# A hybrid decoder block on one core: the mixer's in projection with its column groups in pairs, and seven block products instead of eight for part of them

## The chip, the cores and the metric

The kernel runs on one core of a Trainium2 chip. That core has five engines with instruction streams of their own: TensorE (PE in the profile; its weight loads are PEld), VectorE (DVE), ScalarE (ACT), GpSimd (POOL) and SyncE (SP, which here issues most DMA transfers). Each works through its own list strictly in order and waits at semaphores for the others. The metric is the device time of one execution in microseconds (us).

## The reference, cut to what matters

One layer on 256 tokens of width 2048: a mixer, a cross attention over 256 memory tokens, a gated feed-forward block, each behind an RMS norm and with a residual add. The change lies in the mixer's first product, `proj`:

```python
def hybrid_mixer(h, w_in, ...):
    proj = h @ w_in                       # (256 x 2048) @ (2048 x 11296)
    z, xbc, dt_raw, sc_u, sc_b, sc_c = jnp.split(proj, IN_SPLITS, axis=-1)
    xbc = jax.nn.silu(causal_dwconv(xbc, ssd_conv_w) + ssd_conv_b)
    xs, bm, cm = jnp.split(xbc, ...)
    y = ssd_chunked(xh, dt, a, bm, cm)    # a state space scan, here as 256 x 256 products
    y_ssd = grouped_rmsnorm((y + xh * d_skip) * jax.nn.silu(z), ssd_norm, SSD_GROUPS)
    v = sc_b * causal_dwconv(sc_c * sc_u, sc_conv_w)
    y_sc = grouped_rmsnorm(v, sc_norm, SC_GROUPS)
    return jnp.concatenate([y_ssd, y_sc], axis=-1) @ w_out
```

All arrays are float32.

## The kernel before

**Three products for one.** Each operand of a large product is split into a high part (`fp32r`) and the rest, `hi + lo`, and a block product is three matmuls: hi·hi and lo·hi with the weights' high part (L312, L313 in `tok_mm`), hi·lo with their low part (L316). The weights stream in from memory in chunks of 128 x 1024, which are two feature tiles (a "feature pair") by 512 columns. Each is split when it has landed: ScalarE casts (`h`, L238), VectorE subtracts (`l`, L239). One chunk is then 12 matmuls of 512 columns: two feature tiles, two halves of the tokens (128 each), three matmuls. There are six raw buffers `r`, four of `h` and four of `l`, so a split can be at most four chunks ahead of TensorE.

**The in projection.** Its columns (less 32 that are done apart) are 22 groups of 512. Groups 0 and 1 run together while the input lands; groups 2 to 21 follow one by one, eight chunks each, two chunks to a `unit`. A group has two PSUM accumulators (`a`, four banks in all); the other four banks (`m`, from `msc()`) are lent in turn to the side work.

**Side work.** When a group is summed, its `group_post` starts: scale and evacuate (L338), transpose in blocks (L331), write to memory (`put`) and read back in feature order (`get`), then convolutions, gates, the scan and norms. These are Python generators in a list `procs`; each `unit` calls `step()` once, after its first chunk's matmuls, which moves every one on to its next `yield`. Steps that need TensorE (transposes L717 of a group of `xs`, the scan's products L733 and L735, and others) use banks `m`, which VectorE or ScalarE then read (L720 reads the L717 transposes).

**Who sets the order.** TensorE's and SP's lists stand in the order in which the code is written. VectorE's, ScalarE's and GpSimd's are set once, when the program is built, by a scheduler that may move an instruction far from where it was written. [...]

**Seven products.** Other stages (`wo`, `g`/`u`, `d`) already replace, for some pairs of column groups, the 2 x 2 x 2 block products of a feature pair by seven (a Strassen-Winograd scheme): features in two halves, columns in two groups, tokens in two halves. It needs sums of weight blocks (`pair_sums`: four additions L213 to L216 and three splits L220, L221 a time, on VectorE and ScalarE), sums of token blocks (`token_sums`), four shared PSUM banks `p` for products that go into more than one result, and at the end four additions of these (`p_post`, L938 to L942) and an addition of the correction to each accumulator. `seven_mm` issues 21 matmuls (L990, L991, L993) in three groups: into p[0] and g[0]; into p[3] and p[1]; into p[2], g[1] and u[0].

Of the kernel before, what the change touches and what calls it, by code (L numbers as in the profile page):

```python
# [24 lines left out]
T = 256  # L25
# [5 lines left out]
SEVEN = {n: 3 if n < 10 else 2 for n in range(1, 11)}  # L31
OUT_GAPS = (2, 5, 4, 5)
# [34 lines left out]
def out_order():  # L67

    late = (6, 7, 14, 15)
    return ([(n, c) for n in range(2) for c in range(KT) if c not in late] + [(n, c) for n in range(2) for c in late])  # L70

# [50 lines left out]
def stream_plan():  # L122
# [3 lines left out]
    for n in range(2, 22):  # L126
        p += [(("in", n, c), 1024) for c in range(KT // 2)]
# [8 lines left out]
def trunk(tc, wst, vecs, xp, xtp, mp, mtp, wdt_in, nfin, outp):  # L136
# [9 lines left out]
    with ExitStack() as ctx:  # L146
# [57 lines left out]
        second_of = {part[1]: part[0] for u in out_units() + ffn_units() + down_units() for part in u if len(part) == 2}  # L204
# [129 lines left out]
        def scaled(accs, r):  # L334

            o = [slot() for _ in range(2)]
            for tb in range(2):
                act(o[tb], accs[tb], AF.Identity, scale=r[:, tb:tb + 1])  # L338
            return o
# [40 lines left out]
        def unit(parts, post=None):  # L380
# [192 lines left out]
        def group_post(n, accs):  # L573
            t = turn_blocks(scaled(accs, scales["x"]))
# [15 lines left out]
        def after(k, p):  # L590
            for _ in range(k):
                yield
            yield from p

# [23 lines left out]
        for kt in range(KT):  # L618
            first_unit(kt)

# [231 lines left out]
        def in_units(n, accs, cs):  # L852
            for c in cs:
                unit([([("in", n, k)], lambda k=k: tok_mm(accs, ("in", n, k), side_blocks(xn, 2 * k), (0, 1),
                                                        k == 0, k == KT // 2 - 1)) for k in (c, c + 1)],
                     group_post(n, accs) if c == KT // 2 - 2 else None)

        for n in range(2, len(groups)):
            for one in [] if isinstance(groups[n], tuple) else groups[n]:
                if one[0] == "B" and one[2] > 0:  # L860
                    procs.append(decay(one[2]))
            in_units(n, [acc(), acc()], range(0, KT // 2, 2))
# [68 lines left out]
        shared, seven_a = {}, {}  # L931
        corr = {}

# [19 lines left out]

        def token_sums(key, parts, wide=False):


            xy = fp.tile([128, 1024], F32, tag="f", name=nm("f"))
            w = 512 // len(parts)
            for i, (hi, lo) in enumerate(parts):
# [611 lines left out]
```

## Time and profile before

| | |
|---|---|
| median of 3 runs | 1479.62 us (1479.49 to 1479.84) |
| the profiled execution | 1479.07 us, span of its instructions 1477.3 us |
| TensorE busy | 1466.2 us, 99% |
| VectorE busy | 1212.1 us, 82% |
| ScalarE busy | 864.2 us, 58% |
| DMA moved | 350.91 MB, 238 GB/s on the mean |

The profile is of one execution. A row of a timeline has start, length, engine, line, operation, output tile <- input tiles with shapes, and in brackets how long the engine sat idle before it and on whom it waited. Buffer numbers are left out of names. A row with x4 is four instructions that overlap at their ends, so what one costs in a full list is the distance from start to start. A chain of waits follows the time back from the last instruction, at each step to what released it.

### The profile page before, as it was taken

The page shows a single profiled execution, that of the slowest core. Times are in us where ns is not written, and L with a number is a line of the kernel's source. Part 1 is how long each engine was busy: PE and PEld are TensorE (multiplying, and loading weights), DVE is VectorE, ACT ScalarE, POOL GpSimd, SP SyncE. Part 2 cuts the span into 40 slices and gives each one's busy share as a digit, 9 for nine tenths or more (in the row PEclk, how much of TensorE's full clock was granted, in tenths as well). Part 3 has the DMA queues.
Part 4 walks back from the last instruction along what each step waited for, and adds up shares of the span by engine and source line. Part 5 has one row for each costly group of instructions (what it writes and reads, how often), then busy time and mean ns, then how long its engine had stood idle before and what let it go on. Part 6 is the DMA issues. An engine that isn't in the chain of part 4 may idle for free.

```text
span 1477.3 us, 18842 instructions
## 1 busy us (share of the span) xinstructions
PE 1466.2 (99%) x6592; PEld 1208.1 (82%) x6592; DVE 1212.1 (82%) x1738; ACT 864.2 (58%) x1228; POOL 34.6 (2%) x46
## 2 busy tenths in 40 slices
PE   9999999999999999999999999999999999999997
PEld 7788888888888888888888888888888887888886
DVE  6667777876786775897578999999999998979995
ACT  7467654866664544665466665556655554655663
POOL 0012000101000000000000000000000000000000
PEclk9999999999999999999999999999999999999999
DMA  9877766868667675777658766656676666765553
GB/s 367 273 252 260 264 220 228 289 219 307 228 240 267 198 249 186 254 271 278 226 172 296 263 217 230 214 212 228 229 248 248 206 237 229 269 219 199 195 202 112
DMA packets 151519, 350.91 MB, mean 238 GB/s; under 512 B 11616, under 2 KB 63232, under 8 KB 151424
## 3 DMA queue, kind: packets, MB, share of 16 engines
q1 hardware_dynamic: 142368, 342.83, 66.6%
q10 hardware_dynamic: 9056, 6.87, 1.6%
q8 instruction: 51, 0.84, 0.2%
q14 instruction: 44, 0.36, 0.1%
HBM read 323.40 MB, written 26.26 MB: 237 GB/s over the span
## 4 chain that ended last, share of the span: by engine, by line
PE 98%; DVE 1%; issue 0%; DMA 0%; ACT 0%; DVEq 0%; POOLq 0%; POOL 0%; SPq 0%
PE a L312 27%; PE a L313 26%; PE a L316 26%; PE m L993 3%; PE m L990 3%; PE m L991 3%; PE a L991 2%; PE a L990 2%; PE a L993 2%; PE m L733 1%; PE m L312 0%; PE m L313 0%; PE m L316 0%; PE m L1147 0%; PE m L735 0%
## 5 line engine op out<-in xcount | busy, mean ns | idle before, releaser
L238 ACT CAST h<-r 128x1024 fp32r<-128x1024 f32 (+1 forms) x539 | 562.5, 1048 | 405.2 <-PE a L313 231.8
L239 DVE TENSOR_TENSOR l<-r,h 128x1024 fp32r<-128x1024 f32 (+1 forms) x539 | 650.5, 1216 | 175.0 <-ACT h L238 166.5
L312 PE MATMUL a<-h,s 128*128 128x512 f32 x1735 | 679.3, 392 | 0.1
L313 PE MATMUL a<-h,s 128*128 128x512 f32 x1735 | 675.6, 389 | 0.0
L316 PE MATMUL a<-l,s 128*128 128x512 f32 x1735 | 466.9, 389 | 0.0
L312 PEld LDWEIGHTS a<-h,s 128*128 128x128 f32 x1735 | 326.0, 188 | 69.5 <-issue 2.0
L316 PEld LDWEIGHTS a<-l,s 128*128 128x128 f32 x1735 | 325.6, 188 | 68.1 <-DVE l L239 0.4
L313 PEld LDWEIGHTS a<-h,s 128*128 128x128 f32 x1735 | 326.0, 188 | 66.8
L220 ACT CAST s<-b 128x512 fp32r<-128x512 f32 x94 | 58.0, 618 | 60.9 <-DVE b L213 55.6
L221 DVE TENSOR_TENSOR s<-b,s 128x512 fp32r<-128x512 f32 x94 | 64.6, 687 | 0.1
L331 DVE STREAM_TRANSPOSE b<-s 128x512 f32<-128x512 f32 x62 | 40.7, 690 | 7.0 <-ACT s L338 7.0
L213 DVE TENSOR_TENSOR b<-r,r 128x512 f32<-128x512 f32 x47 | 32.2, 686 | 7.8 <-DMA r<-in_w_dram 7.8
L674 DVE SCALAR_TENSOR_TENSOR t<-t,vec,t 128x255 f32<-128x255 f32 (+2 forms) x72 | 33.0, 489 | 5.8 <-ACT t L671 5.1
L214 DVE TENSOR_TENSOR r<-r 128x512 f32<-128x512 f32 x47 | 32.4, 689 | 0.7
L216 DVE TENSOR_TENSOR r<-b,r 128x512 f32<-128x512 f32 x47 | 32.2, 686 | 0.1
L221 DVE TENSOR_TENSOR s<-r,s 128x512 fp32r<-128x512 f32 x47 | 32.2, 685 | 0.0
L215 DVE TENSOR_TENSOR b<-b,r 128x512 f32<-128x512 f32 x47 | 32.2, 685 | 0.0
L220 ACT CAST s<-r 128x512 fp32r<-128x512 f32 x47 | 29.0, 618 | 4.6 <-DVE r L216 3.2
L993 PE MATMUL m<-s,t 128*128 128x512 f32 x76 | 29.6, 389 | 0.0
L990 PE MATMUL m<-s,t 128*128 128x512 f32 x76 | 29.6, 389 | 0.0
L991 PE MATMUL m<-s,t 128*128 128x512 f32 x76 | 29.6, 389 | 0.0
L338 ACT ACTIVATE s<-a,xr 128x512 f32<-128x512 f32 x42 | 26.5, 681 | 4.2 <-issue 3.7
(240 smaller groups left out, 1241.4 us busy)
## 6 DMA issues: line engine op xcount, KB each, us to landing
r<-in_w_dram SPq DMA_DIRECT2D x535, 512.0 KB, 4.8
w<-b SPq DMA_DIRECT2D x42, 512.0 KB, 3.3
f<-w SPq DMA_DIRECT2D x42, 512.0 KB, 4.9
s<-acsT ACTq DMA_DIRECT2D x24, 256.0 KB, 5.1
s<-in_xt_dram SPq DMA_DIRECT2D x16, 256.0 KB, 7.0
s<-in_mt_dram SPq DMA_DIRECT2D x8, 256.0 KB, 6.3
s<-in_m_dram SPq DMA_DIRECT2D x8, 256.0 KB, 6.1
parked<-s SPq DMA_DIRECT2D x8, 256.0 KB, 8.4
```

Source lines behind the costliest of these rows:

```text
L220: nc.scalar.copy(h, x)
L221: tt(l, x, h.bitcast(F32), ALU.subtract)
L238: nc.scalar.copy(h[:, c], r[:, c])
L239: tt(l[:, c], r[:, c], h[:, c].bitcast(F32), ALU.subtract)
L312: mm(ps[tb], ah, h[:, w], start=first and i == ks[0], stop=False)
L313: mm(ps[tb], al, h[:, w], start=False, stop=False)
L316: mm(ps[tb], blocks(i, tb)[0], l[:, i * 512:i * 512 + 512], start=False, stop=stop and i == ks[-1])
L331: nc.vector.transpose(t[:, tb * 512:tb * 512 + 512], src[tb])
L674: stt(a[:, d:], u[:, 0:T - d], v("cw", 4 * ct + k), a[:, d:], ALU.mult, ALU.add)
L990: mm(ps, ah, bh, start=any(ps is q for q in start), stop=False)
L991: mm(ps, al, bh, start=False, stop=False)
L993: mm(ps, ah, bl, start=False, stop=any(ps is q for q in stop))
```

## The change

Groups 2 to 21 are taken in ten pairs (n, n+1). In the pairs 4, 6, 8, 10, 12 and 14 the feature pairs 0 and 1 are done for both groups together by seven block products. Their order there is: c0 (both groups), chunk 2 of the first group alone, c1 (both groups), then the rest in twos. c0, chunk 2 and c1 call no `step()`. The pairs 2, 16, 18 and 20 keep eight chunks of one group and then eight of the other.

```diff
+IN_SEVEN = range(4, 16, 2)
+def in_units():
+    o = []
+    for n in range(2, 22, 2):
+        g, u = [[("in", n + i, c) for c in range(KT // 2)] for i in range(2)]
+        if n in IN_SEVEN:
+            o += [[(g[0], u[0])], [(g[2],)], [(g[1], u[1])]]
+            k = g[3:] + u[2:]
+        else:
+            k = g + u
+        o += [[(a,) for a in k[i:i + 2]] for i in range(0, len(k), 2)]
+    return o
...
-        def scaled(accs, r):
+        def scaled(accs, r, adds=None):
             o = [slot() for _ in range(2)]
             for tb in range(2):
-                act(o[tb], accs[tb], AF.Identity, scale=r[:, tb:tb + 1])
+                src = accs[tb]
+                if adds is not None:
+                    c, op = adds[tb]
+                    tt(o[tb], src, c, op)
+                    src = o[tb]
+                act(o[tb], src, AF.Identity, scale=r[:, tb:tb + 1])
...
                 if i == 0:
-                    step()
+                    if steps:
+                        step()
                     split_to(last + 3)
...
+            if kt in (8, 10):
+                c = kt // 2 - 4
+                token_sums(("in", c), [(xn[2 * c + k][:, 0:T], xn[2 * c + k][:, T:]) for k in range(2)], True)
...
-        for n in range(2, len(groups)):
-            ...
-            in_units(n, [acc(), acc()], range(0, KT // 2, 2))
+        def in_post(n, p):
+            c11, c21, c12, c22 = [slot() for _ in range(4)]
+            nc.scalar.copy(c11, p[0])
+            tt(c22, p[2], c11, ALU.subtract)
+            tt(c12, p[1], c22, ALU.add)
+            tt(c21, p[3], c22, ALU.add)
+            tt(c22, p[1], c21, ALU.add)
+            in_corr[n] = (c11, ALU.add), (c21, ALU.subtract)
+            in_corr[n + 1] = (c12, ALU.add), (c22, ALU.add)
+        for parts in in_units():
+            keys = [k for part in parts for k in part]
+            for _, n, c in keys:
+                if n not in iaccs:
+                    iaccs[n] = [acc(), acc()]
+                    if len(parts[0]) == 2 and n % 2:
+                        shared["in", n - 1] = [msc() for _ in range(4)]
+                if c == 2:
+                    ...        # start decay() of a group of B columns
+            _, n, c = keys[-1]
+            quiet = len(parts[0]) == 2 or len(parts) == 1 and c == 2
+            post = [group_post(k[1], iaccs[k[1]]) for k in keys if k[2] == KT // 2 - 1]
+            unit([(list(part), lambda part=part: in_mm(part)) for part in parts], None, not quiet)
+            for q in post:
+                next(q)
+                procs.append(q)
+            if len(parts[0]) == 2 and c == 1:
+                in_post(n - 1, shared["in", n - 1])
```

The functions `token_sums` and `seven_mm` are moved up unchanged. Lines of the changed kernel in what follows: L214 loads a chunk, L254 and L255 split it (L238, L239 before), L229 to L237 are `pair_sums` (L213 to L221 before), L328, L329, L332 the plain matmuls (L312, L313, L316), L657, L658, L660 the seven-product matmuls (L990, L991, L993), L788 the transposes of `xs` and L791 VectorE's read of them (L717, L720), L889 and L891 the product and square in `scb_post` (L818, L820), L357 the new addition in `scaled`, L926 to L930 `in_post`. Numbers behind a name tell buffers apart.

**TensorE, from the last chunk of group 5 into c0 of pair 6.** Before, at the comparable place: the end of a chunk of the group behind, two transposes each into `m265` and `m266`, the next chunk.

```order
L316 MATMUL a238_1187<-l260_1287,s60_335 128x512
L316 MATMUL a239_1188<-l260_1287,s60_335 128x512
L717 MATMUL m265_1324<-ident_94,s225_1142 128x128 x2
L717 MATMUL m266_1327<-ident_94,s228_1151 128x128 x2
L312 MATMUL a238_1187<-h261_1290,s66_362 128x512
L313 MATMUL a238_1187<-h261_1290,s66_362 128x512
L312 MATMUL a239_1188<-h261_1290,s66_362 128x512
```

Now, with p[0] = `m323`, p[1] = `m324`, p[2] = `m325`, p[3] = `m326`:

```order
L788 MATMUL m302_1447<-ident_94,s266_1266 128x128 x2
L788 MATMUL m303_1450<-ident_94,s269_1275 128x128 x2
L657 MATMUL m323_1495<-h299_1411,s14_130 128x512
L658 MATMUL m323_1495<-h299_1411,s14_130 128x512
L657 MATMUL a319_1491<-h299_1411,s19_143 128x512
L658 MATMUL a319_1491<-h299_1411,s19_143 128x512
L660 MATMUL m323_1495<-l300_1412,s14_130 128x512
L660 MATMUL a319_1491<-l300_1412,s19_143 128x512
L657 MATMUL m326_1498<-h313_1476,s72_381 128x512
L658 MATMUL m326_1498<-h313_1476,s73_382 128x512
L657 MATMUL m324_1496<-s307_1464,s72_381 128x512
L658 MATMUL m324_1496<-s307_1464,s73_382 128x512
```

Two more rows of p[3] and p[1] (L660) follow, and then p[2]:

```order
L660 MATMUL m326_1498<-l314_1477,s72_381 128x512
L660 MATMUL m324_1496<-s308_1465,s72_381 128x512
L657 MATMUL m325_1497<-s309_1468,s72_381 128x512
L658 MATMUL m325_1497<-s309_1468,s73_382 128x512
L657 MATMUL a320_1492<-s311_1472,s19_143 128x512
```

What moved: the transposes of the side work now stand right ahead of a block that takes all four banks `m`. The banks are lent in turn, so p[1] gets the bank that is free after `m302` has been read and p[2] the one after `m303`. In the built program the first matmul into `m324` waits for the L791 that reads `m302`, and the first into `m325`, the 13th of the block, for the L791 that reads `m303`.

**VectorE at the same place.** Before, the two reads of the transposes (L720) follow each other, between splits and the side work of other groups:

```order
L239 TENSOR_TENSOR l269_1333<-r255_1264,h268_1332 128x1024
L818 TENSOR_TENSOR s169_854<-s169_854,f267_1330 128x512
L818 TENSOR_TENSOR s170_855<-s170_855,f267_1330 128x512
L239 TENSOR_TENSOR l271_1337<-r256_1266,h270_1336 128x1024
L823 TENSOR_TENSOR q274_1373<-q274_1373,q275_1376 128x512
L720 TENSOR_TENSOR s225_1142<-m265_1324,dtn_121 128x256
L720 TENSOR_TENSOR s228_1151<-m266_1327,dtn_121 128x256
```

Now the two L357 stand first (they read the accumulators of group 5 and wait for its last matmul), then splits and transposes, and the sums of c1:

```order
L357 TENSOR_TENSOR s316_1482<-a215_1037,s245_1146 128x512
L357 TENSOR_TENSOR s317_1483<-a216_1038,s246_1147 128x512
L255 TENSOR_TENSOR l329_1523<-r294_1387,h328_1522 128x1024
L347 STREAM_TRANSPOSE b318_1488<-s316_1482 128x512
L347 STREAM_TRANSPOSE b318_1488<-s317_1483 128x512
L255 TENSOR_TENSOR l331_1527<-r301_1427,h330_1526 128x1024
L229 TENSOR_TENSOR b333_1544<-r301_1427,r315_1480 128x512
L791 TENSOR_TENSOR s266_1266<-m302_1447,dtn_121 128x256
```

The list goes on from there with the rest of the sums of c1:

```order
L230 TENSOR_TENSOR r315_1480<-r315_1480 128x512
L231 TENSOR_TENSOR b333_1544<-b333_1544,r315_1480 128x512
L237 TENSOR_TENSOR s335_1550<-b333_1544,s334_1549 128x512
L232 TENSOR_TENSOR r301_1427<-b333_1544,r301_1427 128x512
L237 TENSOR_TENSOR s337_1554<-b333_1544,s336_1553 128x512
L255 TENSOR_TENSOR l341_1562<-r315_1480,h340_1561 128x1024
L237 TENSOR_TENSOR s339_1558<-r301_1427,s338_1557 128x512
L791 TENSOR_TENSOR s269_1275<-m303_1450,dtn_121 128x256
```

What moved: the read of `m303` now stands 15 instructions behind the first L357. At the start of pair 8 the list is the same but for one split, which stands ahead of the L357 there (its L791 stand 6 and 14 instructions behind the first L357). At the starts of pairs 4, 10, 12 and 14 no L791 stands there.

**ScalarE, ahead of c0 of pair 12.** Between the casts of the two chunks of c0 (`h631`, `h645`) stand three loads of activation tables, five of the scan's exponentials (L727, L729) and the two squares L891:

```order
L254 CAST h631_2784<-r611_2696 128x1024
L727 ACT_TABLE_LOAD
L727 ACTIVATE s597_2635<-s597_2635,nacs_122 128x256
L746 ACT_TABLE_LOAD
L746 ACTIVATE s622_2760<-t624_2763 128x256
L746 ACTIVATE s625_2769<-t627_2772 128x256
L817 ACTIVATE s634_2816<-s507_2288 128x256
L729 ACT_TABLE_LOAD
L729 ACTIVATE s598_2637<-s598_2637,nacs_122 128x128
L820 ACTIVATE t635_2820<-s510_2297 128x256
```

Before, the same instructions stood between the casts of plain chunks; the number of table loads in the program, 12, is unchanged.

More of the change, by code (lines that the diff above doesn't have):

```diff
@@ L125, in stream_plan @@
     p += [(("ab", kt), 1024) for kt in range(1, KT)]
-    for n in range(2, 22):
-        p += [(("in", n, c), 1024) for c in range(KT // 2)]
+    p += [(k, 1024) for k in order_of(in_units())]
     p += [(("wo", n, c), 1024) for n, c in out_order()]
@@ L203, in trunk @@
         held, pair_parts = {}, {}
-        second_of = {part[1]: part[0] for u in out_units() + ffn_units() + down_units() for part in u if len(part) == 2}
+        second_of = {part[1]: part[0] for u in in_units() + out_units() + ffn_units() + down_units()
+                     for part in u if len(part) == 2}
         first_of = set(second_of.values())
@@ L378, in trunk, with unit @@
         AHEAD = 6
-        def unit(parts, post=None):
+        def unit(parts, post=None, steps=True):
             first = [index[k] for k in parts[0][0]]
@@ L573, in group_post @@
         def group_post(n, accs):
-            t = turn_blocks(scaled(accs, scales["x"]))
+            t = turn_blocks(scaled(accs, scales["x"], in_corr.pop(n, None)))
             yield
@@ L850, in trunk @@
                       "xs": lambda t, src: xs_post(t // 4, t % 4, src)})
[L852 to L856, printed above, removed]
-        for n in range(2, len(groups)):
-            for one in [] if isinstance(groups[n], tuple) else groups[n]:
-                if one[0] == "B" and one[2] > 0:
-                    procs.append(decay(one[2]))
-            in_units(n, [acc(), acc()], range(0, KT // 2, 2))
+        def in_post(n, p):
[7 more added lines that the diff above has]
+            in_corr[n + 1] = (c12, ALU.add), (c22, ALU.add)
@@ new lines, in trunk, with in_mm @@
+        iaccs = {}
+        def in_mm(part):
+            _, n, c = part[0]
+            if len(part) == 2:
+                g, u, p = iaccs[n], iaccs[n + 1], shared["in", n]
+                seven_mm(part, side_blocks(xn, 2 * c), seven_a["in", c], g, u, p,
+                         p + [g[0], g[1], u[0]] if c == 0 else [], p if c == 1 else [])
+                return
+            start = c == 0
+            if n - n % 2 in IN_SEVEN:
+                start = (1,) if n % 2 and c == 2 else False
+            tok_mm(iaccs[n], part[0], side_blocks(xn, 2 * c), (0, 1), start, c == KT // 2 - 1)
@@ new lines, in trunk @@
+        for parts in in_units():
[6 more added lines that the diff above has]
+                if c == 2:
+                    for one in [] if isinstance(groups[n], tuple) else groups[n]:
+                        if one[0] == "B" and one[2] > 0:
+                            procs.append(decay(one[2]))
+            _, n, c = keys[-1]
[7 more added lines that the diff above has]
+                in_post(n - 1, shared["in", n - 1])
@@ L928, in token_scale @@
             return out
-        shared, seven_a = {}, {}
-        corr = {}
         def p_post(n, p, first=None):
```

75 lines of the change are left out of this document (39 added, 36 removed).

## The prediction

> **What bounds the kernel now.** I read the busy times and the chain of waits first, then the windows of the stage that changes, then start-to-start distances in timelines, since busy shares say nothing of what a list costs when it runs without gaps.
>
> ```profile
> PE 1466.2 (99%) x6592; PEld 1208.1 (82%) x6592; DVE 1212.1 (82%) x1738; ACT 864.2 (58%) x1228; POOL 34.6 (2%) x46
> PE 98%; DVE 1%; issue 0%; DMA 0%; ACT 0%; DVEq 0%; POOLq 0%; POOL 0%; SPq 0%
> ```
>
> TensorE carries 98% of the chain: 11.1 us of the 1477.3 us span are not its own. Matmuls taken away are worth their full time, and every wait put into its list costs its full length. The stage of pairs 4 to 14 lies at about 97 to 367 us, found by counting the matmuls ahead of it; behind it are the four last plain groups and more:
>
> ```profile
> 97.30:367.00 269.70, 269.70 (x1242) 221.39 (x1241) 198.65 (x286) 171.82 (x265) 20.04 (x22) 1.00 0.73 251
> 367.00:502.70 135.70, 135.70 (x633) 110.88 (x632) 101.41 (x158) 77.67 (x114) 3.00 (x3) 1.00 0.70 242
> 850.00:1200.00 350.00, 350.00 (x1546) 289.82 (x1545) 335.89 (x432) 204.40 (x254) 0.00 (x0) 1.00 0.63 224
> ```
>
> Columns: window, busy time and count of PE, PEld, DVE, ACT, POOL, then clock, DMA share, GB/s. In the stage VectorE is busy 198.65 of 269.70 us (74%). From 850 to 1200 us, where seven products are already used, it is busy 96% and TensorE loses nothing. A nearly full VectorE alone is thus no loss; what counts is where its list makes TensorE wait.
>
> What a matmul costs: chunks that follow each other, one with four transposes ahead, and a block of seven products.
>
> ```profile
> 59.05 0.91 PE a L316 x4
> 61.77 0.91 PE a L316 x4
> ...
> 360.62 0.91 PE a L316 x4
> 363.82 0.92 PE a L316 x4
> ```
>
> ```profile
> 863.70 0.39 PE L990 MATMUL m<-h,s 128*128 128x512 f32 x1
> ...
> 868.46 0.39 PE L312 MATMUL a<-h,s 128*128 128x512 f32 x1
> ```
>
> A chunk takes 61.77 - 59.05 = 2.72 us for 12 matmuls, 0.2267 us each. With four transposes in it, it takes 3.20 us, so these are 0.48 us. The 21 matmuls of a seven-block take 4.76 us, again 0.2267 each.
>
> What VectorE's instructions cost in a full list:
>
> ```profile
> 859.46 0.68 DVE L216 TENSOR_TENSOR r<-b,r 128x512 f32<-128x512 f32 x1
> 860.06 0.69 DVE L221 TENSOR_TENSOR s<-b,s 128x512 fp32r<-128x512 f32 x1
> 860.66 1.22 DVE L239 TENSOR_TENSOR l<-r,h 128x1024 fp32r<-128x1024 f32 x1
> 861.79 0.69 DVE L221 TENSOR_TENSOR s<-r,s 128x512 fp32r<-128x512 f32 x1
> 862.40 1.22 DVE L239 TENSOR_TENSOR l<-r,h 128x1024 fp32r<-128x1024 f32 x1
> 863.67 1.29 DVE L1232 TENSOR_TENSOR f<-a,f 128x512 f32<-128x512 f32 x2
> 864.88 1.41 DVE L1249 SCALAR_TENSOR_TENSOR g<-f,fscale,g 128x512 f32<-128x512 f32 x2
> 866.20 1.30 DVE L331 STREAM_TRANSPOSE b<-g 128x512 f32<-128x512 f32 x2
> 867.42 2.32 DVE L239 TENSOR_TENSOR l<-r,h 128x1024 fp32r<-128x1024 f32 x2
> ```
>
> ```profile
> 122.43 1.30 DVE L331 STREAM_TRANSPOSE b<-s 128x512 f32<-128x512 f32 x2
> ...
> 135.41 1.29 DVE L818 TENSOR_TENSOR s<-s,f 128x512 f32<-128x512 f32 x2 [5.97 <-DMA f<-w]
> 136.62 1.22 DVE L239 TENSOR_TENSOR l<-r,h 128x1024 fp32r<-128x1024 f32 x1
> 137.76 0.68 DVE L823 TENSOR_TENSOR q<-q,q 128x512 f32<-128x512 f32 x1
> 138.36 0.75 DVE L720 TENSOR_TENSOR s<-m,dtn 128x256 f32<-128x256 f32 x2
> 139.02 0.42 DVE L825 TENSOR_TENSOR t<-q 128x256 f32<-128x256 f32 x1
> ```
>
> Start to start: an addition or subtraction of 512 columns 0.60, a split 1.14, two additions from an accumulator (L1232, the same form as the new L357) 1.21, two block transposes 1.22, two reads of transposes (L720) 0.66. The second fence also shows a wait in order: group 4's data, turned at 122.43, are back from memory only at 135.41, 13.0 us later, and VectorE idles 5.97 us for them. TensorE was far enough behind not to notice.
>
> **The change part by part.** The sum is made against the profiled 1479.07 us; the median of the runs is 0.55 us above it.
>
> *Matmuls.* Twelve blocks save 3 each: 36 x 0.2267 = -8.16 us. That they are gone is certain: the list has 6352 rows for 6388.
>
> *VectorE's total.* Per block 7 x 0.60 = 4.2 us (four additions, three rests), times 12 is 50.4; per pair four additions in `in_post` and four in `scaled`, 8 x 0.60 = 4.8, times 6 is 28.8. The token sums add about 4. So the six pairs get 79 us on top of 198.65, which is 278 us, while TensorE's time falls to 261.5. Counted start to start the whole list is about 270. The 8 us over are about what the four split buffers let VectorE lead by (three chunks, 8.2 us). This is tight but would pass, as at 850 to 1200. ScalarE gets 36 casts and 6 copies of about 0.6, 25 us on 172: not a bound by its total.
>
> *The start of pair 6.* Set t = 0 at the last matmul of group 5. The first L357 waits for it, so nothing behind it in VectorE's list can run earlier. The matmul into p[2] is due after four transposes (0.48) and 12 matmuls (2.72), at 3.2 us. It waits for the second L791. Up to and with that one VectorE has: two L357 1.21, two splits 2.28, the transposes 1.22, seven additions or subtractions of 512 columns 4.20, a third split 1.14, two L791 0.66, together 10.7 us. TensorE must wait 10.7 - 3.2 = 7.5 us, whatever VectorE had ready. On top, VectorE may reach the L357 late: ahead of it, amid the sums of c0, stand two L889 that wait for group 4's data. These are turned about 2.5 us after that group's last chunk; six chunks of group 5 and about 0.5 us of small matmuls follow (16.8 us). With the 13.0 us of the fence above, the data come 1.3 us ahead of t = 0, and 2.9 us of work then stand ahead of the L357: 1.6 us late. I take 7.5 + 1.6 = +9.1 us, bounds 7.5 and 10.5.
>
> *The start of pair 8.* The same with one split fewer: 9.6 - 3.2 = +6.4 us; no wait for data stands there, bounds 6.4 and 8.
>
> *The start of pair 12.* No L791, but two L889 again, with 5.7 us of list between them and the L357: 5.7 - 1.3 = 4.4 us late. ScalarE's cast of the second chunk stands behind three table loads and behind squares of the same data.
>
> ```profile
> L656 ACT ACT_TABLE_LOAD x4 | 5.1, 1283 | 0.1
> DVE s L818 <- DMA f<-w: 14.3, 4, 6.0
> ```
>
> A load is 1.28 us; the waits for such data were 14.3 us in four places, the longest 6.0. In c0 the matmul into u[0], the 17th, is due at 3.6 and needs the first L357, done at 5.0: 1.4 us. In c1 the low part of its second chunk is due at 4.76 + 2.72 + 10 x 0.2267 = 9.75, plus those 1.4. VectorE has 9.8 us of list from the L357 to it and began 4.4 late, so 14.2 against 11.15: 3.1 more. I take +4.5. The lower bound is 0.9, from totals alone (47.7 us of VectorE's list in pair 10 against 43.9 of TensorE's, less the 2.9 that the L357 has to spare); the upper is 6, the longest such wait.
>
> *c1 of pairs 4, 10 and 14.* There 9.5 us of list stand against the 9.75: +1.0 together, bounds 0 and 3.
>
> *The start.* The token sums, 4 us in small pieces, now stand between the first splits:
>
> ```profile
> 10.69 1.23 DVE L239 TENSOR_TENSOR l<-r,h 128x1024 fp32r<-128x1024 f32 x1 [1.04 <-ACT h L238]
> ...
> 11.96 0.73 PE L316 MATMUL a<-l,s 128*128 128x512 f32 x2
> ```
>
> The third chunk's rest ends at 11.92 and is used at 11.96, so no room is left there: +0.3, bounds 0 and 1.
>
> *At no cost.* Pausing side work: the read-back of a second group starts some 12 us later; its posts wait in `procs` and the plain pairs, where VectorE has 34 us idle of 135.7, take them up. SP's list has the same 690 transfers; a `put` waits for the turn just written ahead of it, but the chunks behind it are loaded six ahead. `in_post` holds the four banks until its last addition; the next side step that wants one stands a chunk (2.72 us) later and needs p[0] or p[2] first. Bounds 0 and +1 each.
>
> Sum: -8.16 + 9.1 + 6.4 + 4.5 + 1.0 + 0.3 = +13.1, so 1492.2 in the profile's terms and, with the 0.55, about 1492.7; I say 1493. The bounds add to +6.6 and +20.3.
>
> **The rivals.**
>
> *The clock.* The first wait of pair 6 is for p[1], due at 0.48 + 8 x 0.2267 = 2.3 us and released by the first L791 at 5.6 to 7.2 us: up to 4.9 us idle, then four matmuls, then some 4 us idle more.
>
> ```profile
> 1466.00:1470.00 4.00, 2.93 (x16) 2.35 (x14) 1.93 (x6) 1.42 (x5) 0.00 (x0) 1.00 0.75 253
> 1470.00:1477.30 7.30, 0.00 (x0) 0.00 (x0) 1.70 (x5) 1.45 (x4) 0.56 (x1) 0.76 0.44 148
> ```
>
> ```profile
> 1.81 2.93 PE L446 MATMUL m<-U 128*128 128x256 f32 x6 [1.81 <-POOL U L442]
> 4.82 0.79 PE L312 MATMUL a<-h,s 128*128 128x512 f32 x1
> ...
> 6.17 0.40 PE L313 MATMUL a<-h,s 128*128 128x512 f32 x1
> ```
>
> At the end of the span the clock falls: a mean of 0.76 over 7.30 us is 3.5 us at half, so it halved at 1473.8, some 4.9 us after the last matmul at 1468.9. At the start matmuls take 0.79 us and reach 0.40 only at 6.17, 4.4 us after the first one. A halving would then cost about 4.4 / 2 = 2.2 us, one to three times in pairs 6 and 8: +2.2 to +6.6, so 1495 to 1499. Against it: the waits are at the edge of the 4.9 us. The Trainium skill, "TensorE: Matmul & The Clock Gate", Part 1, puts the idle window at about 3.4 us and the time at half rate after it at about as much; by its window three of the four waits could halve the clock, and by its figures that would be an estimated 1.7 us each. The trace agrees in kind and shows a longer time; nothing in it shows an idle stretch between 1 and 4.9 us. Chance 0.35.
>
> *VectorE is on time everywhere.* Its lateness at pairs 6 and 12 hangs on when data return. If they return 5 us earlier, only 7.5 + 6.4 - 8.16 = +5.7 stays: 1485.4. Against it stand the 13.0 us. Chance 0.15.
>
> *Only totals count (faster).* If the two L791 in pairs 6 and 8 were done within 3.2 us of the last matmul, the waits would vanish and the 8.2 us lead would cover VectorE's total: 1479.6 - 8.2 = 1471.4. For it speaks the stage at 850 to 1200 us; against it that VectorE's list is in order and the L357 cannot run before the group ends. Chance 0.02.
>
> *About the same.* The waits at half their price, because the L357 or the splits behind it cost less than their rows: 1479.6 + 7 - 8.2, near 1478.5. Chance 0.04.
>
> **How the numbers follow.** Main forecast 0.44 (1488 to 1495), clock 0.35, on time 0.15, same 0.04, faster 0.02. The range for 8 in 10 goes from 1485.5, just at the on-time case, to 1502, the upper bounds together or the main sum with the clock's upper end. Within 0.2% (3.0 us), about what a measurement here can tell from no change, lies the half-price case, 0.04; faster 0.02; slower 0.94.
>
> **What the profile after would show.** In the table of waits, TensorE waiting for L791 in two places, for 9 and 6 us; shares of VectorE in the chain rising by those; idle stretches of TensorE at the starts of pairs 6, 8 and 12 and next to none at 4, 10 and 14; outside 97 to 360 us, nothing changed. Matmuls of 0.79 us behind the waits and a clock under 1.00 in their windows would show the clock's rival. Wrong would be the forecast if the wait at L791 is under 5 us, or if TensorE stalls in the plain pairs behind.

## The result, and the profile after

| | before | changed |
|---|---|---|
| median | 1479.55 us | 1507.02 us (1505.35 to 1508.21) |
| profiled execution, span | 1479.07, 1477.3 | 1505.35, 1503.5 |
| ratio, 95% interval | | 1.0184 (1.0172 to 1.0196) |

Slower, as forecast, but by 27.5 us where 13.4 were forecast, and 5 us beyond the upper end of the range. The busy times and the chain of the changed kernel:

```profile
PE 1467.5 (98%) x6556; PEld 1204.5 (80%) x6556; DVE 1291.5 (86%) x1884; ACT 888.5 (59%) x1272; POOL 34.5 (2%) x46
PE 78%; DVE 6%; issue 1%; DMA 1%; ACT 0%; DVEq 0%; POOLq 0%; POOL 0%; SPq 0%; ACTq 0%
```

TensorE had 98% of the chain and has 78%; VectorE had 1% and has 6%. These shares say on which engine the chain runs, not how much was lost: the 26.2 us that the span grew are 2% of it. TensorE's busy time in the first line is no smaller, though 36 matmuls are gone: some of those left ran slowly, as shown below. The table of waits (total, number of times, longest, in us) has two entries of some size for TensorE's matmuls, which the kernel before did not have:

```profile
PE m L657 <- DVE s L791: 17.3, 4, 7.8
...
PE m L660 <- DVE l L255: 6.5, 7, 1.2
```

The first is the wait for a bank that has to be freed by a read of xs_post's transposes, at the starts of pairs 6 and 8; the second is that for the rest (the low part `l`) of c0's or c1's second chunk. The timeline of TensorE at pair 6, then at pair 8:

```profile
144.84 0.39 PE L658 MATMUL m<-h,s 128*128 128x512 f32 x1
153.00 0.79 PE L657 MATMUL m<-s,s 128*128 128x512 f32 x1 [7.77 <-DVE s L791]
153.59 0.63 PE L658 MATMUL m<-s,s 128*128 128x512 f32 x1
...
154.44 0.63 PE L660 MATMUL m<-s,s 128*128 128x512 f32 x1
158.22 0.77 PE L657 MATMUL m<-s,s 128*128 128x512 f32 x1 [3.14 <-DVE s L791]
```

```profile
204.15 0.39 PE L658 MATMUL m<-h,s 128*128 128x512 f32 x1
206.65 0.50 PE L657 MATMUL m<-s,s 128*128 128x512 f32 x1 [2.11 <-DVE s L791]
...
207.44 0.40 PE L660 MATMUL m<-s,s 128*128 128x512 f32 x1
212.14 0.77 PE L657 MATMUL m<-s,s 128*128 128x512 f32 x1 [4.30 <-DVE s L791]
```

Start to start, less one matmul of 0.2267, the stalls are 7.9 and 3.35 us at pair 6 (the last at the slow rate, 0.43 a matmul) and 2.3 and 4.5 at pair 8. Between 153.59 and 154.44 two matmuls take 0.85 us, 0.43 each: half rate. The stage as a whole, and single stretches of 3.41 us at those two places (columns as in the windows ahead: window, its length, busy time and count of PE, PEld, DVE, ACT and POOL, the clock, DMA share, GB/s):

```profile
97.30:367.00 269.70, 245.15 (x1092) 196.45 (x1091) 246.92 (x375) 173.57 (x262) 13.26 (x15) 0.96 0.64 219
```

```profile
146.77:150.18 3.41, 0.00 (x0) 1.00 0.81 238
150.18:153.60 3.42, 0.60 (x2) 0.50 0.72 230
153.60:157.01 3.41, 1.47 (x4) 0.50 0.00 0
157.01:160.42 3.41, 2.20 (x5) 0.50 0.60 165
160.42:163.84 3.42, 3.42 (x9) 0.50 0.79 296
163.84:167.25 3.41, 3.41 (x16) 1.00 0.44 154
```

(The second fence gives PE alone, then the clock, DMA share and GB/s.) From 150.18 to 163.84 us the clock is 0.50; 9 matmuls touch the last 3.42 us of it, and 16 touch the next 3.41 at full clock. Another 6.83 us at half rate follow at 208.21.

With the stalls between starts of successive matmuls added up over the whole stage, the 26.2 us that the span grew come apart like this:

| part | forecast | measured |
|---|---|---|
| 36 matmuls less | -8.16 | -8.16 |
| start of pair 6 | +9.1 | +11.3 |
| start of pair 8 | +6.4 | +6.7 |
| start of pair 12 | +4.5 | +3.6 |
| c0 and c1 of pairs 4, 10, 14 | +1.0 | +4.9 |
| matmuls at half clock | a rival | about +5.3 |
| start of the kernel | +0.3 | +0.4 |
| the rest | | about +2.2 |

The start is read where matmuls of the same kind stand in both lists up to 97 us: those of the changed kernel come 0.36 us later. Of the rest, 0.6 us are two small waits behind the stage, at 402 and 832 us, and about 1.1 us come from the matmul that follows each wait, which takes 0.34 us from start to start instead of 0.23.

### The profile page after: what moved, and what is told of

The parts are those of the page before. It is cut to its first block, busy times and chain, and to the rows that moved or that the text cites. A ratio compares the mean times of both kernels' runs of the same rounds, so it can differ in the third digit from the quotient of the medians.

```text
span 1503.5 us, 18981 instructions
## 1 busy us (share of the span) xinstructions
PE 1467.5 (98%) x6556; PEld 1204.5 (80%) x6556; DVE 1291.5 (86%) x1884; ACT 888.5 (59%) x1272; POOL 34.5 (2%) x46
## 4 chain that ended last, share of the span: by engine, by line
PE 78%; DVE 6%; issue 1%; DMA 1%; ACT 0%; DVEq 0%; POOLq 0%; POOL 0%; SPq 0%; ACTq 0%
PE a L328 20%; PE a L329 20%; PE a L332 20%; PE m L660 3%; PE m L657 3%; PE m L658 3%; PE a L658 2%; PE a L657 2%; PE a L660 2%; DVE l L255 1%; DVE s L237 1%; DMA f<-w 1%; DVE b L347 0%; PE m L804 0%; DVE r L230 0%
## 5 line engine op out<-in xcount | busy, mean ns | idle before, releaser
L254 ACT CAST h<-r 128x1024 fp32r<-128x1024 f32 (+1 forms) x539 | 562.3, 1046 | 408.2 <-PE a L329 200.7
L255 DVE TENSOR_TENSOR l<-r,h 128x1024 fp32r<-128x1024 f32 (+1 forms) x539 | 649.2, 1215 | 133.3 <-ACT h L254 128.6
L328 PE MATMUL a<-h,s 128*128 128x512 f32 x1639 | 643.1, 392 | 0.0
L329 PE MATMUL a<-h,s 128*128 128x512 f32 x1639 | 639.5, 390 | 0.1
L332 PE MATMUL a<-l,s 128*128 128x512 f32 x1639 | 441.8, 390 | 0.3 <-DVE l L255 0.2
L328 PEld LDWEIGHTS a<-h,s 128*128 128x128 f32 x1639 | 308.5, 188 | 65.7 <-issue 1.8
L332 PEld LDWEIGHTS a<-l,s 128*128 128x128 f32 x1639 | 307.9, 188 | 65.1 <-DVE l L255 1.1
L329 PEld LDWEIGHTS a<-h,s 128*128 128x128 f32 x1639 | 308.5, 188 | 63.5 <-DVE s L995 0.5
L236 ACT CAST s<-b 128x512 fp32r<-128x512 f32 x118 | 72.8, 618 | 80.5 <-DVE b L229 75.0
L237 DVE TENSOR_TENSOR s<-b,s 128x512 fp32r<-128x512 f32 x118 | 81.0, 686 | 0.3 <-ACT s L236 0.2
L229 DVE TENSOR_TENSOR b<-r,r 128x512 f32<-128x512 f32 x59 | 40.4, 684 | 8.2 <-DMA r<-in_w_dram 8.2
L230 DVE TENSOR_TENSOR r<-r 128x512 f32<-128x512 f32 x59 | 40.6, 687 | 0.9
L237 DVE TENSOR_TENSOR s<-r,s 128x512 fp32r<-128x512 f32 x59 | 40.4, 684 | 0.0
L660 PE MATMUL m<-l,s 128*128 128x512 f32 x80 | 32.1, 401 | 5.7 <-DVE l L255 5.7
L657 PE MATMUL m<-s,s 128*128 128x512 f32 x42 | 17.7, 421 | 17.3 <-DVE s L791 17.3
L657 PE MATMUL m<-h,s 128*128 128x512 f32 x80 | 31.7, 396 | 1.6 <-ACT h L254 1.6
L658 PE MATMUL a<-h,s 128*128 128x512 f32 x80 | 31.6, 396 | 0.0
```

Source lines behind the costliest of these rows:

```text
L230: tt(u[:, a], u[:, a], u[:, b], ALU.add)
L236: nc.scalar.copy(h, x)
L237: tt(l, x, h.bitcast(F32), ALU.subtract)
L254: nc.scalar.copy(h[:, c], r[:, c])
L255: tt(l[:, c], r[:, c], h[:, c].bitcast(F32), ALU.subtract)
L328: mm(ps[tb], ah, h[:, w], start=first and i == ks[0], stop=False)
```

## The experiments

All ratios below are against the kernel before, run on the same chip. Theory A: the loss comes from TensorE's waits for L791, the half clock behind them included. Rival B: VectorE has as much to do in the stage as TensorE, and the waits only show where it runs out. Others are named where they come up. Line numbers shift by one or a few where an edit adds lines.

### No side step ahead of c0

```diff
-            quiet = len(parts[0]) == 2 or len(parts) == 1 and c == 2
+            quiet = len(parts) == 1
```

> Edit: no side step in any unit of one chunk, so not in the last chunk of group 5 or 7 either; the four transposes of xs_post then no longer stand between group 5 (7) and the c0 of pair 6 (8). Theory A (TensorE's two waits at each of these places come from banks lent to the transposes and read late in VectorE's list): both waits (11.3 us at pair 6, 6.5 us at pair 8) and the half clock behind them (about 5.3 us) go; what VectorE is late then shows at u[0] and in c1, 0 to 3 us: 1484 to 1488. Rival B (VectorE simply has more to do in the stage than TensorE, so the waits only move to other places): 1500 to 1507.

1494.56 us, ratio 1.0107 (1.0090 to 1.0123). Neither theory's range. TensorE waits nowhere for L791 any more, and 12.5 of the 23 us that theory A gave to these waits are won. The rest is in waits that were hidden or smaller before; the largest group, from the waits between 97 and 357 us:

```profile
PE m L660 <- DVE l L255: 9.5, 9, 1.2
```

Every c1 of the six pairs now waits for the rest of its second chunk, and c0 of pairs 4, 8 and 12 does so too. In addition the clock still halved twice, for 3.41 us each. So A names a real cost, but not what limits the kernel once that is removed.

### The reads ahead in VectorE's list

```diff
+            with tc.high_priority():
-            tt(xd, pt[:, 0:T]...
+                tt(xd, pt[:, 0:T]...
```

> Edit: the two reads of the transposes (L791) get the scheduler's high priority, so that they stand ahead of the last rest of c0, the second split and the two L357 in VectorE's list; the transposes stay where they are on TensorE. Theory A: p[1] and p[2] no longer wait for them; the L357 are now about 5 us late, so u[0] waits some 2 us, and c1 2 to 4 us in the two pairs; no half clock: 1487 to 1492. Rival C (a side step at this place costs as such, through the transposes and the held banks, whenever they are read): 1500 or more.

1491.56 us, ratio 1.0082 (1.0067 to 1.0097): inside A's range. The transposes stand where they stood; only the two reads moved ahead in VectorE's list, and 15.5 us are gone. So rival C, that the side step costs as such, falls. Theory A expected no half clock; one stretch of 3.41 us remained, at 204.35 us. The same waits for L255 are left:

```profile
PE m L660 <- DVE l L255: 10.2, 9, 1.6
```

### Spare matmuls in the waits

```diff
...
+                for _ in range(spare[turn]):
+                    mm(g[1], raw(0, 0)[0], gh[:, a], start=True, stop=True)
```

(ahead of the second and third group of products in c0 of pairs 6 and 8; g[1] is overwritten by its first product later)

> Edit: spare matmuls into the bank of g[1], which its first product overwrites later: in pair 6 30 ahead of the second group of products and 12 ahead of the third, in pair 8 8 and 16; they fit inside the waits (6.8 of 7.9, 2.7 of 3.35, 1.8 of 2.3 and 3.6 of 4.3 us). Theory D (the half clock is a price of its own, for idle time): the clock stays 1.00 at 150 to 164 and 208 to 215 us, the waits stay, and 5.3 us go: 1501 to 1503. Rival E (behind the waits VectorE sets the pace anyway, so that matmuls at half clock cost nothing): 1506 to 1508.

1501.36 us, ratio 1.0146 (1.0131 to 1.0161), 5.7 us less than the changed kernel. The windows at the two starts, first of the changed kernel, then of this one:

```profile
145.00:165.00 20.00, 9.08 (x23) 6.58 (x23) 18.09 (x31) 10.68 (x21) 1.65 (x1) 0.66 0.57 183
203.00:216.00 13.00, 6.59 (x22) 4.75 (x21) 8.76 (x14) 4.69 (x7) 0.00 (x0) 0.74 0.52 171
```

```profile
145.00:165.00 20.00, 18.04 (x73) 14.39 (x72) 18.18 (x29) 13.31 (x25) 0.00 (x0) 0.91 0.55 185
203.00:216.00 13.00, 12.71 (x57) 10.16 (x56) 9.57 (x15) 5.67 (x8) 0.00 (x0) 1.00 0.41 132
```

The mean clock rises from 0.66 to 0.91 and from 0.74 to 1.00, while TensorE does 66 matmuls more than needed. In pair 8 no half clock is left; in pair 6 one stretch of 3.41 us is, which lies on the spare matmuls. The half clock is thus a price of its own, theory D, though that had expected full clock at both places; rival E, that VectorE sets the pace behind the waits anyway, would have left the time at 1506 to 1508.

### The write of a group by GpSimd, and the loads ahead of it

```diff
-            nc.sync.dma_start(w.rearrange("t p k -> p t k"), ...
+            nc.gpsimd.dma_start(w.rearrange("t p k -> p t k"), ...
```

> Edit: the write of a turned group (put, L365) is issued by GpSimd instead of SP, so no load of a chunk stands behind it in SP's list. Theory F (VectorE reaches the L357 of pair 6 late because the load of c0's second chunk stood behind this write, which waited 13 us for the turn): the idle 1.3 us of VectorE ahead of c0's sums goes, the sums begin 1.3 to 3 us earlier and the wait for p[1] shrinks by as much: 1504 to 1506. Rival G (VectorE's own list is the cause, the load comes in time enough): 1506.5 to 1507.5.

1512.47 us, ratio 1.0226 (1.0211 to 1.0241): slower, which neither expected. The edit took the write off SP's list and put it behind GpSimd's masks, which wait for data of their own. The rows of GpSimd and of VectorE:

```profile
142.92 1.38 POOL L714 TENSOR_SCALAR_AFFINE_SELECT s<-s 128x256 f32<-128x256 f32 x1
144.26 0.73 POOL L365 DMA_DIRECT2D w<-b  x1
```

```profile
151.55 1.29 DVE L889 TENSOR_TENSOR s<-s,f 128x512 f32<-128x512 f32 x2 [3.10 <-DMA f<-w]
...
155.10 1.28 DVE L357 TENSOR_TENSOR s<-a,s 128x512 f32<-128x512 f32 x2
```

The write was issued at 144.26 instead of 134.87, its data came back late, VectorE idled 3.10 us for it ahead of the L357, and the wait at p[1] grew to 10.1 us. The same edit cost pair 4 as well: ScalarE idled 3.19 us for data read back, three table loads followed, and TensorE waited 3.6 us for a cast at 102.54, with half clock behind it. So the total says nothing on SP, but the place shows that time lost ahead of the L357 reappears at p[1]. A cleaner edit leaves the write on SP and moves one load ahead of it:

```diff
                 if i == 0:
+                    load_to(last + AHEAD)
                     if steps:
                         step()
```

> Edit: in every unit the load of the sixth chunk ahead is written before the side step instead of behind it; so the load of c0's second chunk of pair 6 stands ahead of the write of group 4 (put) in SP's list. Theory F (this load is why VectorE reaches the L357 of pair 6 later than forecast): VectorE's idle 1.3 us ahead of c0's sums goes and the wait for p[1], 7.9 us, falls to 6 to 7: 1505 to 1506. Rival G (the load isn't the cause, the list ahead is): wait of 7.5 us or more, 1507.

1505.66 us, ratio 1.0176 (1.0161 to 1.0191). The total moved by about 1 us, which by itself tells little; the place tells it. First SP and VectorE in the changed kernel, then TensorE and VectorE with the load first:

```profile
134.87 0.38 SPq L365 DMA_DIRECT2D w<-b  x1
135.35 1.71 SPq L214 DMA_DIRECT2D r<-in_w_dram  x2
```

```profile
140.54 0.69 DVE L229 TENSOR_TENSOR b<-r,r 128x512 f32<-128x512 f32 x1 [1.32 <-DMA r<-in_w_dram]
...
147.28 1.28 DVE L357 TENSOR_TENSOR s<-a,s 128x512 f32<-128x512 f32 x2
...
152.53 0.42 DVE L791 TENSOR_TENSOR s<-m,dtn 128x256 f32<-128x256 f32 x1
...
157.65 0.42 DVE L791 TENSOR_TENSOR s<-m,dtn 128x256 f32<-128x256 f32 x1
```

```profile
151.58 0.80 PE L658 MATMUL m<-s,s 128*128 128x512 f32 x1 [6.13 <-DVE s L792]
```

```profile
145.84 1.28 DVE L357 TENSOR_TENSOR s<-a,s 128x512 f32<-128x512 f32 x2
```

In the changed kernel the load of c0's second chunk was issued right behind the write, half a microsecond after it, and the write had waited until 134.87 for its turn. With the load ahead, the sums start without idle time, and the wait at p[1] falls from 7.9 to 6.3 us. Theory F holds, for 1.65 us of the lateness. From 133.68 to 145.84 us VectorE has no idle stretch in this run, so the 2.8 us by which the L357 are still late are the length of its own list.

### More room between c0 and c1

```diff
-            o += [[(g[0], u[0])], [(g[2],)], [(g[1], u[1])]]
-            k = g[3:] + u[2:]
+            o += [[(g[0], u[0])], [(g[2],)], [(g[3],)], [(g[1], u[1])], [(g[4],)]]
+            k = g[5:] + u[2:]
```

(and no step in single units)

> Edit: as in the run without a step ahead, and two single chunks (g2, g3) instead of one between c0 and c1 in all six pairs. That run kept a wait of 1.1 to 1.4 us in c1 of each of the six pairs, 7.8 us together, for the rest of the second chunk (L660 behind L255). Theory H (c1 stands too close behind c0 for VectorE's list): these six waits go, the others stay: 1485 to 1488 (from 1494.6). Rival B (VectorE has as much work in the stage as TensorE, so the time shows up at the next place, c0): 1492 to 1496.

1507.43 us, ratio 1.0189 (1.0174 to 1.0204). Both ranges missed: the waits for L791 came back at other pairs.

```profile
282.72 0.39 PE L658 MATMUL m<-h,s 128*128 128x512 f32 x1
293.99 0.77 PE L657 MATMUL m<-s,s 128*128 128x512 f32 x1 [10.88 <-DVE s L791]
```

This is pair 12, with 24 matmuls between the transposes and c0; pair 14 lost 7.6 us in the same way. Two experiments that changed which pairs are by seven found it at pair 10 and again at pair 12.

```diff
-IN_SEVEN = range(4, 16, 2)
+IN_SEVEN = (4, 10, 12, 14)
```

> Edit: seven products only in pairs 4, 10, 12 and 14; pairs 6 and 8 by eight products, still paired. Theory A (the loss is in the two starts and the half clock behind them): 11.3 + 6.5 + 5.3 us of waits go, 2.7 us of matmuls come back, from 1507.0 to 1483 to 1488. Rival B (VectorE's total): it also leaves 25 us of VectorE's work out, so waits of pairs 10 to 14 shrink as well: 1478 to 1482.

1491.01 us, ratio 1.0075 (1.0058 to 1.0092), above both ranges. With 6 and 8 plain, the side work meets pair 10 instead:

```profile
240.73 0.76 PE L657 MATMUL m<-s,s 128*128 128x512 f32 x1 [2.30 <-DVE s L791]
...
245.85 0.77 PE L657 MATMUL m<-s,s 128*128 128x512 f32 x1 [3.08 <-DVE s L791]
```

```diff
-IN_SEVEN = range(4, 16, 2)
+IN_SEVEN = (4, 8, 12)
```

(with the gap, and no step in single units)

> Edit: seven products only in pairs 4, 8 and 12, with a plain pair between, no step in single units, two single chunks between c0 and c1. Matmuls save 18 x 0.2267 = 4.1 us. Rival B, VectorE's work over several pairs as the cause of what is left: a plain pair between gives VectorE back its lead, waits of 0 to 2 us in all: 1476 to 1478, faster than before. Theory H', each pair has its price, since some 10 us of VectorE's list must pass between the last matmul of a group and c1: 1 to 2 us a pair stay, 1479 to 1482.

1498.66 us, ratio 1.0130 (1.0115 to 1.0146), above both ranges: 11.6 us at pair 12 for L791, with 13.65 us of half clock behind it. Three waits in plain chunks, of 0.7, 1.2 and 3.0 us, came on top.

What the places have in common is not that the transposes stand directly ahead of c0. It is that the step which wrote them was the last one ahead of the pause. xs_post writes its read one step later, and that step is the first one behind c1. In VectorE's list the read then stands among or behind the sums of c1, while c0 needs all four banks.

### Banks not lent across the pause

```diff
+            while hold[0]:
+                yield
             pt = msc()
```

(the same ahead of yp = msc(); hold[0] is true in the last unit ahead of a unit of pairs of chunks)

> Edit: the order of units and steps of the changed kernel, but a side task does not take a bank of the four (the transposes L788 of xs_post, the products L804) in the last step ahead of c0; it takes it in the first step behind c1. The runs with the gap and without pairs 6 and 8 showed the waits for L791 at other pairs, always where the step that wrote the transposes was the last one ahead of the pause, however many chunks lay between. Theory A' (the bank is lent across the pause, since its read is written one step later, behind the pause): no wait for L791 at any pair; the waits of 1.1 to 1.4 us in c0 and c1 stay, as in the run with the early read: 1488 to 1493. Rival C' (the transposes are only one of several side tasks that collide here): some other wait over 3 us takes their place, 1497 or more.

1490.68 us, ratio 1.0075 (1.0061 to 1.0088), in the range of theory A'. No wait for L791 is left in the stage, and no other wait over 3 us. What is left of size is again the rest of a second chunk:

```profile
PE m L660 <- DVE l L255: 9.9, 9, 2.5
```

Next the same with the gap of two chunks:

```diff
+            o += [[(g[0], u[0])], [(g[2],)], [(g[3],)], [(g[1], u[1])], [(g[4],)]]
```

> Edit: as in the run that holds the banks, and two single chunks instead of one between c0 and c1, all six pairs. Theory H (c1 too close behind c0): the waits in c1, 7 to 8 us with their share of half clock, go and nothing takes their place: 1482 to 1486. Rival B (VectorE's work of the stage is as long as TensorE's): they come back in c0 or in the chunks behind: 1488 to 1493.

1487.90 us, ratio 1.0059 (1.0045 to 1.0073). The waits for L255 fall from 9.9 to 2.7 us, but waits for L357, for ScalarE's casts and more half clock stand in their place: only 2.8 us are won. H expected 1482 to 1486, B 1488 to 1493; the time lies 0.1 us below B's range and 1.9 above H's. It speaks for B, that VectorE's work in the stage is as long as TensorE's, but doesn't show it.

And with three pairs only:

```diff
+IN_SEVEN = (4, 8, 12)
```

> Edit: the same as the run that holds the banks with two chunks between c0 and c1, but seven products only in pairs 4, 8 and 12. Matmuls save 4.1 us. Rival B: the plain pairs between give VectorE its lead back, 0 to 2 us of waits are left: 1475.5 to 1478, faster than before. Theory H' (a price for each pair, wherever it stands): 1479 to 1482.

1483.37 us, ratio 1.0025 (1.0016 to 1.0035). Three pairs save 4.1 us of matmuls and lose 8, mostly in single waits of 0.5 to 1.9 us, one of them in a plain pair. A plain pair between didn't give VectorE its lead back, as B in this form expected; the price per pair is nearer to the truth, and even above H'.

### Pairs without seven products

```diff
-IN_SEVEN = range(4, 16, 2)
+IN_SEVEN = ()
```

> Edit: no pair by seven products; groups still run in pairs as units of two chunks and the first step of a group's post is written at once. Every theory so far puts the whole loss on the seven products and the pause: 1479 to 1480.5, as before. Rival P (the new order of the posts costs by itself): 1482 or more.

1482.29 us, ratio 1.0023 (1.0014 to 1.0032), in rival P's range. So pairing and the immediate first step cost 2.9 us without any seven products: the start costs 0.5 (the token sums are still made there), and one plain chunk at 367 us waits 2.2 behind a VectorE that idled for a read-back.

```profile
369.13 1.20 PE L332 MATMUL a<-l,s 128*128 128x512 f32 x4 [2.07 <-DVE l L255]
```

```profile
365.72 1.29 DVE L872 TENSOR_TENSOR u<-f,f 128x512 f32<-128x512 f32 x2 [8.12 <-DMA f<-w]
```

The changed kernel has no such wait at this place, so the 2.2 are not a part of its sum; they show how a shift of the side work alone moves a wait onto TensorE.

### VectorE's work taken away, and moved to GpSimd

Both runs stand on the kernel that holds the banks and has the gap.

```diff
-            tt(f[:, a], g[:, a], u[:, a], ALU.add)
...
-            tt(g[:, a], f[:, b], g[:, b], ALU.add)
```

(for the in projection alone; casts and rests stay)

> Edit: as in the run with held banks and two chunks between c0 and c1 (1487.9), and the four additions of each block of the in projection (L229 to L232) are left out: the rests and casts behind them are made of the weights as they are, so this kernel's products are not those of the reference. VectorE has 12 x 4 x 0.60 = 28.8 us less to do in the stage, nothing else changes. Theory B (VectorE's work of the stage sets what is left): the waits of 15 us between 97 and 357 us, their half clock with them, fall under 4: 1473 to 1477. Rival K (they come from single late pieces, read-backs and ScalarE's casts): 1481 to 1486.

1474.84 us, ratio 0.9969 (0.9957 to 0.9981). The stage from 97 to 357 us, with the four additions and without:

```profile
97.30:357.00 259.70, 250.37 (x1125) 200.70 (x1124) 251.20 (x384) 176.13 (x271) 16.01 (x16) 0.99 0.69 241
```

```profile
97.30:357.00 259.70, 257.87 (x1184) 210.73 (x1183) 237.94 (x361) 185.83 (x289) 16.15 (x22) 1.00 0.74 256
```

VectorE falls from 251.2 to 237.9 us busy and TensorE rises from 250.4 to 257.9 of 259.7. (The work taken away is more than the difference, since the kernel without the additions gets further in the same window.) Of some 16 us of stalls 4 are left: with the four additions gone, the kernel keeps most of what it saved in matmuls. That is theory B's range, and rival K's, 1481 to 1486, is missed. One thing the run doesn't separate: the additions also stood in a chain ahead of the casts and rests of each block, so without them each block is ready earlier. The longest wait of the base, 2.7 us for a cast of ScalarE at pair 12, is 0.4 here. Whether VectorE's total or this chain sets what is left is therefore not shown.

```diff
+            add = gtt if key[0] == "in" else tt
-            tt(f[:, a], g[:, a], u[:, a], ALU.add)
+            add(f[:, a], g[:, a], u[:, a], op=ALU.add)
```

> Edit: the same base, and these four additions by GpSimd instead of VectorE, 48 additions of 512 columns on an engine with 34.6 us of work in the span. By theory B it takes the 28.8 us off VectorE: 1474 to 1478, faster than before, if an addition takes about 1 us there (the masks L718 of 512 columns take 0.6 to 1.6) and isn't late. Rival G' (it is late: in GpSimd's list the masks L714 that wait for their data stand ahead of the sums of pairs 6 and 12, or an addition takes 2 us or slows VectorE down): waits at p[1], 1484 or more.

1507.68 us, ratio 1.0193 (1.0178 to 1.0208). The additions on GpSimd, and two groups on VectorE in the stage (busy, mean ns), here and then in the base:

```profile
L230 POOL TENSOR_TENSOR b<-r,r 128x512 f32<-128x512 f32 x12 | 21.8, 1813 | 100.8 <-DMA r<-in_w_dram 52.5 <-DVE l L256 19.4 <-DVE t L746 15.3
```

```profile
L256 DVE TENSOR_TENSOR l<-r,h 128x1024 fp32r<-128x1024 f32 x84 | 116.5, 1396 | 7.1 <-ACT h L255 7.0
L746 DVE SCALAR_TENSOR_TENSOR t<-t,vec,t 128x253 f32<-128x253 f32 (+2 forms) x37 | 24.1, 685 | 1.0 <-ACT t L743 1.0
```

```profile
L255 DVE TENSOR_TENSOR l<-r,h 128x1024 fp32r<-128x1024 f32 x90 | 108.2, 1220 | 0.9 <-ACT h L254 0.8
...
L745 DVE SCALAR_TENSOR_TENSOR t<-t,vec,t 128x255 f32<-128x255 f32 (+2 forms) x36 | 16.0, 477 | 0.5 <-ACT t L742 0.5
```

An addition takes 1.6 to 1.8 us there in mean against 0.68 on VectorE, the four of a block stand in a chain, and VectorE's own instructions get longer meanwhile: the split from 1220 to 1396 ns, the short multiply-add from 477 to 685. The trace shows that it is the overlap: of the splits in the stage, the 59 that no addition of GpSimd overlaps take 1214 ns in mean, the 24 others 1806. Rival G' holds, with an addition of nearly 2 us and a slower VectorE. No version that computes all of the reference beat the kernel before.

## Why the prediction was wrong

The direction and the mechanism were right: the matmuls saved are -8.16 as forecast, and the largest loss is the wait for L791 at pairs 6 and 8. Pair 8, whose price was read off a list of rows (6.4), came out at 6.7. Pair 12 (4.5) measured 3.6, inside its bounds; the start 0.4, inside its own. Four steps failed.

**The lateness at pair 6.** The term was 7.5 for the list plus 1.6 for VectorE's late arrival; it measured 11.3. The L357 began at 147.28, about 4.5 us after the last matmul of group 5, not 1.6. The 1.6 was worked out from the two L889 that wait for data; those had their data in time. What was late was c0's sums, and the step that missed it is "At no cost", where SP's list was dismissed because the chunks are loaded six ahead. The one load that counted stood behind the write that waited. Moving it ahead took 1.65 us off the wait; the rest of the lateness, about 1.3 us beyond the forecast, came with VectorE busy throughout, so its list ahead of the L357 was longer than the working had it.

**The half clock.** It stood as a rival with a chance of 0.35 and not in the sum. It happened at both places and lasted longer than one stretch at a time: 13.65 and 6.83 us, about 5.3 us of matmuls, inside the 2.2 to 6.6 that the rival named. The spare matmuls won 5.7. What failed is the step "against it": the waits were taken to be at the edge of 4.9 us. The Trainium skill's rule ("TensorE: Matmul & The Clock Gate", Part 1) of about 3.4 us of idling was nearer than the 4.9 us read off the end of the span; the runs agree with it in length (3.41 us) and are harsher (a stretch with 1.2 us of matmuls in it was enough), as said in the last section. The range's upper end stood for the upper bounds together or for the clock, but not for a late pair 6 with the clock on top, and that is what came: 13.1 + 5.3 from the clock, 2.2 more at pair 6 and 3.9 more in c1, less 0.9 at pair 12, is 23.6 of the 26.2 us that the span grew. The +20.3 of the upper bounds also leaves out the +1 of each of the three terms at "At no cost". With them it is +23.3, about 1503, and still 4 us short.

**c1.** The term was 1.0 for pairs 4, 10 and 14, from 9.5 us of list against 9.75; it measured 4.9, of which 1.2 in c0 of pair 4. With c1 one chunk further off, and the banks held, the waits for L255 in the stage fell from 9.9 to 2.7 us, so it is this distance that they hang on. The working had VectorE on time at each group's end; that it came late in these pairs too is argued, from 246.92 us busy of 269.70, and not shown.

**VectorE's total.** The size was right (79 us forecast; over the whole span VectorE's busy time rose from 1212.1 to 1291.5), but "tight but would pass" was wrong. Once the waits for L791 are gone, VectorE is 97% busy from 97 to 357 us and TensorE loses some 16 us there; with 28.8 us of its work removed, 4, though that run, as said, also shortens the chain ahead of each block. The stretch from 850 to 1200 us, where a VectorE that is busy 96% costs nothing, was the wrong witness; why it passes there and not here was not tested.

The changed kernel's pause itself, costed at nothing, is what puts the read of the transposes behind c1. The prediction had the place from the order of the two kernels and priced it rightly there, without its reason; hence the expectations with the gap, without pairs 6 and 8 and with every second pair missed, because moving units or pairs moved the collision and didn't remove it.

## What to carry to other kernels

Where side work is paused, look at what it holds at that moment: a bank lent in the last step ahead of the pause comes back one step after it, whatever stands between. When waits leave TensorE busy for less than half of some 3.4 us, add the slow clock behind them to the sum and don't keep it as an alternative. Expect an engine that would be 97% busy to cost something, even if another stage of the same kernel runs at 96% without loss.

## What the runs showed of the hardware

The clock went by a fixed raster. In all runs every stretch at half clock inside the span lasts a multiple of 3.41 us, and so does every stretch between two of them (143.36 us is 42 of them). What goes with it is how busy TensorE was in one cell of the raster: after a cell with few matmuls the next one runs at half rate. Three pairs of cells, from the changed kernel, the run with the early read, and the run with three pairs (the columns of the first windows):

```profile
204.80:208.21 3.41, 1.20 (x4) 0.67 (x4) 3.41 (x7) 1.19 (x2) 0.00 (x0) 1.00 0.33 127
208.21:211.62 3.41, 0.00 (x0) 0.00 (x0) 3.18 (x6) 1.51 (x3) 0.00 (x0) 0.50 0.01 2
```

```profile
200.94:204.35 3.41, 1.75 (x7) 0.80 (x5) 3.41 (x6) 3.18 (x6) 0.00 (x0) 1.00 0.02 6
204.35:207.77 3.42, 3.10 (x7) 2.48 (x8) 3.14 (x4) 2.25 (x3) 0.00 (x0) 0.50 0.60 165
```

```profile
273.71:277.12 3.41, 1.64 (x8) 1.34 (x8) 3.38 (x6) 3.36 (x5) 1.54 (x1) 1.00 0.88 312
277.12:280.54 3.42, 3.42 (x17) 2.84 (x16) 3.42 (x4) 3.39 (x6) 0.82 (x1) 1.00 0.72 252
```

Over all runs, without the last 25 us of each span, of the cells that ran at full clock themselves, 18 had TensorE busy for less than 1.6 of the 3.41 us, and each was followed by half clock; between 1.6 and 1.8 us it was 5 of 11; above that, none. In the last 25 us it was 16 of 17 below 1.6 us, the exception at 1.56. So no idle stretch of 3.4 us is needed: in the second pair TensorE idled 1.7 us of the cell, in two pieces under 1 us each, and that was enough. What else decides around 1.6 to 1.8 us stays open.

The raster also accounts for the 4.9 us that the prediction read off the end of the span. In the kernel before, the clock halves at 1473.77, so the cell ahead of it begins at 1470.36 and holds no matmul; the last one, at 1468.9, lies in the cell before that, 1.5 us ahead of its end, and 1.5 + 3.41 is 4.9.

GpSimd's additions of 512 columns took 1.6 to 1.8 us in mean (1.28 to 3.08 singly) and went with VectorE's instructions being up to 44% longer in mean (477 to 685 ns, a group of three shapes). Only some were affected: splits that overlapped an addition took 1806 ns against 1214, while the nine L358 in the stage that overlapped one, and which read an accumulator, took 675 ns, as long as the others (679).
